# An opening by quarters of the inner dimension, in a written order, and narrower modulation products

## The chip, the cores and the metric

The kernel runs on one core of one Trainium2 chip. Times are device microseconds of one execution; the time before is the median of three runs, 1925.92 us (1925.78 to 1932.32).

## What is computed

Two sequences, a prompt of 256 tokens and a sample of 512, each with a conditioning vector `c`, go through a trunk of two layers with 1024 channels:

```python
for l in range(DEPTH):
    mod = jax.nn.silu(c) @ adaln_w[l] + adaln_b[l]           # 1024 -> 6 x 1024
    sh1, sc1, g1, sh2, sc2, g2 = [t[:, None, :] for t in jnp.split(mod, 6, axis=-1)]
    h = rmsnorm(x, norm_g[l, 0]) * (1 + sc1) + sh1
    y = mlstm_mixer(h, ...) if l % 2 == 0 else swa_mixer(h, ...)
    x = x + g1 * y
    h = rmsnorm(x, norm_g[l, 1]) * (1 + sc2) + sh2
    x = x + g2 * conv_ffn(h, ...)
return rmsnorm(x, final_g)
```

The mixer of layer 0 is a bidirectional mLSTM with four heads. From `h` it takes q, k, v and an output gate (1024 columns each) and 16 gate columns; the gates go through a log-sigmoid, cumulative sums and running maxima, whose results weigh the scores q k^T of each head. All of it is in float32.

## The kernel before

Activations lie transposed, channels on the 128 partitions in eight chunks (`KC`), tokens along the free dimension: the prompt at columns 0 to 255, the sample at 256 to 767. A float32 operand of a large matmul is split into a rounded high part (ScalarE) and the rest (VectorE) by `fp_copy_split`, L221, and each product is done as three: high x high, high x low, low x high. Modulated activations are held split in `hh` and `hl` (the tiles zh and zl in the profile), weights in `whi` and `wlo`. All matmuls but transposes and the feed-forward's are recorded at L219. A weight half (`load`, 512 KB) holds 128 output columns of all eight chunks: one "tile" of a projection is 24 products for a sequence.

The program is written in Python and ordered per engine by a scheduler that works with a cost model; the order in the text is a priority, not the order of execution. Tiles are taken from pools with a fixed number of buffers: six large `slab`s, five `raw` landing buffers, three `whi` and three `wlo`, four PSUM banks `ps` and four `pa`.

The opening is `first`, L1281. It loads x by ranges (sample columns 256 to 511, 512 to 767, then the prompt) and, between them, the 8 MB of the first 2048 columns of layer 0's modulation matrix (shift and scale of the mixer) in sixteen pieces of 128 rows by 1024 columns. `adaln`, L354, multiplies each piece by `silc`, silu(c) of both sequences padded to 32 columns, in two products of 512 columns, each into a strip of 32 partitions of one PSUM bank; all eight chunks of the inner dimension have to be summed before the bank is copied, transposed and added to the bias as `mod` and `gain`. `Norm`, L85, squares on ScalarE, adds six chunks on GpSimd, sums over partitions on PE (L119), takes the power on GpSimd (L126) and spreads the factor with PE (L131); `scaled`, L485, multiplies x by it, and `modulate`, L490, applies gain and shift and splits. When that is done for the sample, `window`, L276, runs the first three tiles (gates, two of head 0's q) over both ranges of the sample and then the prompt. Head 0's k (two tiles) and v (`gemmN`, L297) follow in `mlstm`, L559, and beside them the chain of the gates: table loads, scans (L599 to L606), a trip through DRAM (`mrows`) and masks on GpSimd (L626), without which no score of head 0 can be weighed.

The other modulation columns are worked off beside the heads, as generators advanced at fixed places: `fillp` does layer 0's remaining 4096 columns on PE with `adaln`; `fill` does layer 1's on VectorE with `adaln_v`, L415, one step being two operations of 128x1024.

Of the kernel before, what the change touches and what calls it, by code (L numbers as in the profile page):

```python
# [140 lines left out]
class Net:  # L141
# [103 lines left out]

    def halves(self, u):
        for h in range(2):
            yield h, self.split(self.load(u, h))

    def step(self, gen, n=1):  # L250
        for _ in range(n):
            next(gen, None)

# [7 lines left out]
    def gemmT_steps(self, w, q, act=None):  # L261
        s0, s1 = SEQS[q]
        wh, wl = (t.rearrange("p (k m) -> p k m", k=KC) for t in w)
        ps = self.ps()
        o = ps[:, : s1 - s0]
        for k in range(KC):
            if act is None:
                ah, al = self.hh[:, k, s0:s1], self.hl[:, k, s0:s1]
            else:
                ah, al = act(k, s0, s1)  # L270
            self.mm(o, wh[:, k], ah, k == 0, False)
            self.mm(o, wh[:, k], al, False, False)
            self.mm(o, wl[:, k], ah, False, k == KC - 1)
            yield o

    def window(self, items):  # L276

        bank = {}
        for rng in RANGES:
# [3 lines left out]
            for i, (w, consume) in enumerate(items):  # L283
# [10 lines left out]
                if c1 == s1:  # L294
                    consume(q, bank[i, q][:, : s1 - s0])

# [57 lines left out]
    def adaln(self, l, th, first=False):  # L354
        nc = self.nc
        hold = None

        def fetch(i):
            nonlocal hold
            k, h = divmod(i, 2)  # L360
            c0 = th * 2048 + h * 1024
            src = self.io["adaln_w"][l, k * P : (k + 1) * P, c0 : c0 + 1024]
            if k < 2 or not first:
                return self.raw(src)
            z = (i - 4) % 3
            if z == 0:
                hold = self.slab([P, 3, 1024])
            nc.sync.dma_start(hold[:, z], src)
            return hold[:, z]

        if not first:
            part = fetch(0)
            yield
        ps = self.ps()
        for i in range(2 * KC):
            k, h = divmod(i, 2)
            cur = fetch(i) if first else part
            if not first and i < 2 * KC - 1:
                part = fetch(i + 1)
            for g in range(2):  # L380
                r0 = 32 * (2 * h + g)
# [3 lines left out]
            if i < 2 * KC - 1 and (h or not first):  # L385
                yield
        sb = self.stg.tile([P, 2, 256], F32, tag="raw", name=self.nm("sb"), bufs=5)
        sb = [sb[:, z] for z in range(2)]
        nc.vector.tensor_copy(sb[0], ps[:, :256])
        nc.scalar.copy(sb[1], ps[:, 256:])  # L390
        pt = self.ps()
        for b in range(4):
            nc.tensor.transpose(
                pt[:, b * P : (b + 1) * P], sb[b // 2][:, (b % 2) * P : (b % 2 + 1) * P], self.ident
            )
        src = pt.rearrange("p (b g s) -> p g b s", b=4, g=4)[:, :, :, 0:2]
        dst = self.mod[l][:, th * 16 : (th + 1) * 16, :].rearrange("p (g b) s -> p g b s", g=4)
        ab = self.cst(AB + 48 * l + 16 * th, 16).rearrange("p (g b) -> p g b", g=4)
        for s in range(2):
            nc.vector.tensor_tensor(dst[:, :, :, s], src[:, :, :, s], ab, ALU.add)  # L400
        i = {0: 0, 2: 1}.get(th)
        if i is not None:
            c0 = 8 if i == 0 else 32
            for s in range(2):
                nc.vector.scalar_tensor_tensor(
                    self.gain[l][i][:, :, s],
                    self.mod[l][:, c0 : c0 + 8, s],
                    1.0,
                    self.cst(NG + (2 * l + i) * 8, 8),
                    ALU.add,  # L410
                    ALU.mult,
# [77 lines left out]

    def modulate(self, xt, rng, l, i):  # L490
        c0, c1, q = rng
        for c in range(KC):
            x = xt[c // 4][:, c % 4, c0:c1]
            self.nc.vector.tensor_scalar(
                x, x, self.gain[l][i][:, c, q : q + 1], self.mod[l][:, 24 * i + c, q : q + 1], ALU.mult, ALU.add
            )
            self.fp_copy_split(self.hh[:, c, c0:c1], self.hl[:, c, c0:c1], x)
# [61 lines left out]
    def mlstm(self, pool, gw, xt):  # L559
# [22 lines left out]
        qt0 = self.slab([P, 2, 2, T], R)  # L582
# [3 lines left out]
        norm = Norm(self, xt, PROMPT, self.modulated(0, 0), KC)  # L586
        for c in range(KC):
            norm.square(c)
        self.start(PROMPT, norm.stages())
        self.window(ws)  # L590
# [846 lines left out]
```

## Time and profile before

| | |
|---|---|
| median of the runs | 1925.92 us |
| profiled execution | 1921.48 us, span 1919.4 us |
| PE busy | 1836.2 us (96%) |
| DVE busy | 1387.2 us (72%) |
| ACT busy | 909.8 us (47%) |
| POOL busy | 559.6 us (29%) |
| chain that ended last | PE 80%, DVE 6%, issue 5%, DMA 3%, POOL 3% |

The profile covers one execution. A row of a timeline gives the start and the length in us, the engine, the source line, the operation, the tiles written and read, their shapes, how many records were merged, and in brackets how long the engine had been idle and what released it. PE is the matmul unit, PEld its weight loads, DVE VectorE, ACT ScalarE, POOL GpSimd. A float32 product on PE that is not split beforehand leaves two records, and some records can be missing. Matmuls are pipelined: the distance between two starts is what one costs, not the length in its row.

### The profile page before, as it was taken

The page shows a single profiled execution, that of the slowest core. Times are in us where ns is not written, and L with a number is a line of the kernel's source. Part 1 is how long each engine was busy: PE and PEld are TensorE (multiplying, and loading weights), DVE is VectorE, ACT ScalarE, POOL GpSimd, SP SyncE. Part 2 cuts the span into 40 slices and gives each one's busy share as a digit, 9 for nine tenths or more (in the row PEclk, how much of TensorE's full clock was granted, in tenths as well). Part 3 has the DMA queues.
Part 4 walks back from the last instruction along what each step waited for, and adds up shares of the span by engine and source line. Part 5 has one row for each costly group of instructions (what it writes and reads, how often), then busy time and mean ns, then how long its engine had stood idle before and what let it go on. Part 6 is the DMA issues. An engine that isn't in the chain of part 4 may idle for free.

```text
span 1919.4 us, 28838 instructions
## 1 busy us (share of the span) xinstructions
PE 1836.2 (96%) x11142; PEld 1662.5 (87%) x11142; DVE 1387.2 (72%) x2243; ACT 909.8 (47%) x1826; POOL 559.6 (29%) x438
## 2 busy tenths in 40 slices
PE   7999999999999999999999999999899999999997
PEld 4977786888988899999999998779898999999996
DVE  4765566686589867777777765774798777777776
ACT  3444433343456444444444554773565444444443
POOL 2101001022253433333331311342533333333324
PEclk9999999999999999999999999999999999999998
DMA  8344456446212222222222321122222222222211
GB/s 327 107 149 133 148 167 211 134 146 220 83 55 78 69 64 67 66 66 67 67 69 86 99 90 52 40 87 78 82 73 66 66 66 67 73 70 67 66 34 66
DMA packets 63956, 183.41 MB, mean 96 GB/s; under 512 B 6135, under 2 KB 23799, under 8 KB 63820
## 3 DMA queue, kind: packets, MB, share of 16 engines
q1 hardware_dynamic: 63820, 181.58, 29.7%
q8 instruction: 87, 1.43, 0.3%
q14 instruction: 49, 0.40, 0.1%
HBM read 175.13 MB, written 6.43 MB: 95 GB/s over the span
## 4 chain that ended last, share of the span: by engine, by line
PE 80%; DVE 6%; issue 5%; DMA 3%; POOL 3%; ACT 2%; SPq 0%; POOLq 0%; ACTq 0%; DVEq 0%
PE pa L219 25%; PE ps L219 22%; PE ps L1050 10%; PE ps L1051 10%; PE ps L1052 10%; PE pa L908 2%; DMA raw<-in_adaln_w_dram 1%; DVE wlo L226 1%; DVE slab L517 1%; POOL nt L107 1%; PE pa L1050 1%; PE pa L1051 1%; ACT whi L225 1%; PE pa L1052 1%; DMA slab<-in_x_dram 1%
## 5 line engine op out<-in xcount | busy, mean ns | idle before, releaser
L225 ACT CAST whi<-raw 128x1024 fp32r<-128x1024 f32 x243 | 254.6, 1049 | 413.0 <-PE pa L219 203.5
L226 DVE TENSOR_TENSOR wlo<-raw,whi 128x1024 fp32r<-128x1024 f32 x243 | 335.3, 1381 | 132.9 <-ACT whi L225 131.4
L219 PE MATMUL pa<-slab,whi 128*128 128x256 f32 (+1 forms) x1472 | 344.7, 331 | 4.8 <-DVE slab L517 4.8
L219 PEld LDWEIGHTS pa<-slab,whi 128*128 128x128 f32 x1472 | 251.1, 188 | 31.8 <-DVE slab L517 6.3
L517 DVE SCALAR_TENSOR_TENSOR slab<-pa,mod,slab 128x256 f32<-128x256 f32 (+1 forms) x368 | 207.4, 592 | 68.8 <-PE pa L219 68.6
L219 PE MATMUL ps<-zh,whi 128*128 128x256 f32 (+2 forms) x688 | 227.6, 334 | 7.4 <-ACT whi L225 4.9
L219 PE MATMUL pa<-slab,wlo 128*128 128x256 f32 (+1 forms) x736 | 233.3, 329 | 0.0
L219 PE MATMUL ps<-zh,wlo 128*128 128x256 f32 (+2 forms) x688 | 227.5, 333 | 3.3 <-DVE wlo L226 3.3
L219 PE MATMUL ps<-zl,whi 128*128 128x256 f32 (+2 forms) x688 | 228.7, 334 | 0.7 <-DVE zl L480 0.7
L1050 PE MATMUL ps<-zh,whi 128*128 128x384 f32 x504 | 171.2, 340 | 17.7 <-ACT ps L1113 16.7
L1052 PE MATMUL ps<-zh,wlo 128*128 128x384 f32 x504 | 169.4, 336 | 0.1
L1051 PE MATMUL ps<-zl,whi 128*128 128x384 f32 x504 | 169.4, 336 | 0.0
L1081 POOL TENSOR_TENSOR raw<-raw,raw 128x512 f32<-128x512 f32 x44 | 60.1, 1366 | 307.5 <-DVE wlo L226 262.4
L219 PEld LDWEIGHTS pa<-slab,wlo 128*128 128x128 f32 x736 | 138.3, 188 | 12.9 <-DVE wlo L226 0.6
L219 PEld LDWEIGHTS ps<-zh,whi 128*128 128x128 f32 x688 | 130.5, 191 | 21.9 <-ACT whi L225 6.5
L219 PEld LDWEIGHTS ps<-zh,wlo 128*128 128x128 f32 x688 | 131.0, 191 | 16.6 <-DVE wlo L226 4.4
L219 PEld LDWEIGHTS ps<-zl,whi 128*128 128x128 f32 x688 | 131.2, 191 | 11.6 <-issue 1.7
L1202 POOL TENSOR_TENSOR slab<-slab 128x772 f32<-128x772 f32 x44 | 87.6, 1991 | 178.9 <-DVE slab L1153 177.8
L1152 DVE SCALAR_TENSOR_TENSOR slab<-slab,cstt,slab 128x771 f32<-128x771 f32 x88 | 107.0, 1218 | 26.7 <-ACT slab L1150 26.7
L436 DVE SCALAR_TENSOR_TENSOR ada<-raw,silc,ada 128x1024 f32<-128x1024 f32 x84 | 109.5, 1336 | 18.4 <-DMA raw<-in_adaln_w_dram 18.4
L1153 DVE SCALAR_TENSOR_TENSOR slab<-slab,cstt,slab 128x771 f32<-128x771 f32 x88 | 121.0, 1376 | 0.7
L1050 PEld LDWEIGHTS ps<-zh,whi 128*128 128x128 f32 x504 | 94.7, 188 | 25.7 <-ACT ps L1113 21.8
(273 smaller groups left out, 4191.9 us busy)
## 6 DMA issues: line engine op xcount, KB each, us to landing
raw<-in_w_dram SPq DMA_DIRECT2D x206, 512.0 KB, 3.7
raw<-in_adaln_w_dram SPq DMA_DIRECT2D x84, 512.0 KB, 4.5
slab<-in_x_dram SPq DMA_DIRECT2D x12, 512.0 KB, 8.3
slab<-in_adaln_w_dram SPq DMA_DIRECT2D x12, 512.0 KB, 10.3
slab<-mrows SPq DMA_DIRECT2D x8, 384.0 KB, 5.1
xs<-slab SPq DMA_DIRECT2D x6, 512.0 KB, 2.9
bt<-brow SPq DMA_DIRECT2D x16, 192.0 KB, 3.1
slab<-xs SPq DMA_DIRECT2D x6, 512.0 KB, 8.1
```

Of the source, the lines that this page charges most:

```text
L219: self.nc.tensor.matmul(out, lhsT, rhs, start=start, stop=stop)
L225: nc.scalar.copy(hi, src)
L226: return nc.vector.tensor_tensor(lo, src, hi.bitcast(F32), ALU.subtract)
L436: stt(acc[:, s], row, w, acc[:, s], ALU.mult, ALU.add)
L517: self.nc.vector.scalar_tensor_tensor(x, o, self.mod[l][:, gc + c, q : q + 1], x, ALU.mult, ALU.add)
L1050: mm(o, wh[:, k], hi[k], start=start and k == 0, stop=False, skip_group_check=True)
L1051: mm(o, wh[:, k], lo[k], start=False, stop=False, skip_group_check=True)
L1052: mm(o, wl[:, k], hi[k], start=False, stop=k == 3, skip_group_check=True)
L1081: tt(q[0], q[2], q[0], ALU.subtract)
L1152: stt(y[:, 1:], u[:, :-1], w(0), y[:, 1:], ALU.mult, ALU.add)
L1153: stt(y[:, :-1], u[:, 1:], w(2), y[:, :-1], ALU.mult, ALU.add)
L1202: nc.gpsimd.tensor_tensor(y, y, yrow[:, j], ALU.mult)
```

## The change

The first 2048 modulation columns come from a second copy of the matrix, `ada0`, packed on the host so that quarter z (four loads of 512 KB) holds all rows for channels 256z to 256z+255 of shift and scale. For each quarter `opening` does `adaln_z` (eight products of 512 columns in four strips, a copy, four products with `sel` that add up the strips and transpose), modulates and splits two chunks of the sample, and does these two chunks' products of the first three tiles, all 512 columns of the sample at once. Then come the prompt's norm, two more tiles (head 0's k) of the sample, and outside of the written part the five tiles of the prompt. PE, ACT and DVE keep the order of the text in `opening`. The x loads of the sample and all quarters with the first weights are issued ahead. `window` stays for layer 1.

The remaining columns of layer 0 go through `adaln_g`: four groups of 1024 columns instead of two of 2048, a step being a piece of 128x1024 as before, but in four products of 256 columns in four strips instead of two of 512 in two. Steps of `fill` move: none in head 0's values, one more at the second block of each sequence's outputs in each head. `modulated` queues a chunk's low part behind the next chunk's product, and the prompt's scores are split in one piece.

```diff
+    def apart(self, src, pool):
+        w = [[pool.tile([P, 640], R, tag="PT", name=self.nm("wp"), bufs=8)[:, :512] for _ in range(2)] for _ in range(2)]
+        for j in range(2):
+            self.fp_copy_split(w[0][j], w[1][j], src[:, 512 * j : 512 * (j + 1)])
+        return w
...
+    def products(self, o, w, ks, cols):
+        for k in ks:
+            ah, al = self.hh[:, k, cols], self.hl[:, k, cols]
+            self.mm(o, w[0][k], ah, k == 0, False)
+            self.mm(o, w[0][k], al, False, False)
+            self.mm(o, w[1][k], ah, False, k == KC - 1)
+
+    def opening(self, xt, units, loads, pool, consume):
+        nc = self.nc
+        sample, prompt = (slice(*s) for s in SEQS)
+        ws, bank = [], []
+        for rng in RANGES[:2]:
+            Norm(self, xt, rng, self.scaled).run()
+        for z in range(4):
+            self.adaln_z(z, units[z], pool)
+            cs = (2 * z, 2 * z + 1)
+            xs = [xt[c // 4][:, c % 4, sample] for c in cs]
+            for c, x in zip(cs, xs):
+                nc.vector.tensor_scalar(
+                    x, x, self.gain[0][0][:, c, 0:1], self.mod[0][:, c, 0:1], ALU.mult, ALU.add
+                )
+            for c, x in zip(cs, xs):
+                self.fp_copy_split(self.hh[:, c, sample], self.hl[:, c, sample], x)
+            for i in range(3):
+                if z == 0:
+                    bank.append(self.ps())
+                    ws.append(self.blocks(self.split(loads[i]) if i else self.apart(loads[i], pool)))
+                self.products(bank[i], ws[i], cs, sample)
+        norm = Norm(self, xt, PROMPT, self.modulated(0, 0))
+        for c in range(KC):
+            norm.square(c)
+        stages = norm.stages()
+        next(stages)
+        for i in range(2):
+            w = self.load(U_MIN + 1, i)
+            ws.append(self.blocks(self.apart(w, pool) if i else self.split(w)))
+        for i in range(3):
+            consume[i](0, bank[i])
+        bank += [self.ps() for _ in range(2)]
+        self.products(bank[3], ws[3], range(4), sample)
+        next(stages)
+        self.products(bank[3], ws[3], range(4, KC), sample)
+        consume[3](0, bank[3])
+        for _ in stages:
+            pass
+        self.products(bank[4], ws[4], range(KC), sample)
+        consume[4](0, bank[4])
+        return ws
...
+    def adaln_z(self, z, units, pool):
+        nc = self.nc
+        ps = self.pa()
+        for k in range(KC):
+            r0 = 32 * (k % 4)
+            self.mm(ps[r0 : r0 + 32], self.silc[:, k, :], units[k // 2][:, k % 2], k < 4, k > 3)
+        sb = pool.tile([P, 640], F32, tag="E", name=self.nm("sb"), bufs=2)
+        nc.scalar.copy(sb[:, :512], ps)
+        pt = self.pa()[:, :8]
+        for b in range(4):
+            self.mm(pt[:, 2 * b : 2 * b + 2], sb[:, b * P : (b + 1) * P], self.sel, True, True)
+        src = pt.rearrange("p (i b s) -> p i b s", i=2, b=2)
+        for i in range(2):
+            c = 8 * i + 2 * z
+            ab = self.cst(AB + c, 2).unsqueeze(2).to_broadcast([P, 2, 2])
+            nc.vector.tensor_tensor(self.mod[0][:, c : c + 2, :], src[:, i], ab, ALU.add)
...
+    def adaln_g(self, l, grp):
...
+        for k in range(KC):
+            cur = part
+            if k < KC - 1:
+                part = fetch(k + 1)
+            for g in range(4):
+                r0 = 32 * g
                 self.mm(
-                    ps[r0 : r0 + 32, :], self.silc[:, k, :], cur[:, g * 512 : (g + 1) * 512], k == 0, k == KC - 1
+                    ps[r0 : r0 + 32, :256], self.silc[:, k, :], cur[:, g * 256 : (g + 1) * 256], k == 0, k == KC - 1
                 )
...
-            for c in range(KC):
-                t = self.tmp([P, c1 - c0])
-                sh = self.mod[l][:, 24 * i + c, q : q + 1]
-                nc.vector.scalar_tensor_tensor(t, x(c), self.gain[l][i][:, c, q : q + 1], pr, ALU.mult, ALU.mult)
-                hi, lo = self.hh[:, c, c0:c1], self.hl[:, c, c0:c1]
-                nc.scalar.activation(hi, t, AF.Identity, bias=sh)
-                nc.vector.scalar_tensor_tensor(lo, t, sh, hi.bitcast(F32), ALU.add, ALU.subtract)
+            ts = []
+            for c in range(KC + 1):
+                if c < KC:
+                    ts.append(self.tmp([P, c1 - c0]))
...
+                if c:
+                    b = c - 1
+                    self.behind = nc.vector.scalar_tensor_tensor(
+                        self.hl[:, b, c0:c1], ts[b], self.mod[l][:, 24 * i + b, q : q + 1],
+                        self.hh[:, b, c0:c1].bitcast(F32), ALU.add, ALU.subtract,
+                    )
...
-        ws = [(gw, gates)] + [(w, keep(qt0, 0, c)) for c, w in self.halves(U_MIN)]
-        self.load_x(io["x"], RANGES[2:], xt)
...
-        self.start(PROMPT, norm.stages())
-        self.window(ws)
-        nc.scalar.preload_act_table_set("natural_log_exp_and_others")
+        with self.tc.manual_schedule(engines={eng.PE, eng.Activation, eng.DVE}):
+            ws = opening(consume)
+        behind = self.behind
+        self.tc.keep_in_program_order(
+            nc.scalar.preload_act_table_set("natural_log_exp_and_others")
+        )
+        for w, f in zip(ws, consume):
+            o = self.ps()[:, :256]
+            self.products(o, w, range(KC), slice(*SEQS[1]))
+            f(1, o)
...
+                    if i == 1:
+                        with self.tc.issue_after(behind.ins):
+                            self.step(self.fill)
...
-        xt = self.load_x(x, RANGES[:1])
-        ada = self.adaln(0, 0, True)
-        steps = lambda n: [next(ada, None) for _ in range(n)]
-        Norm(self, xt, RANGES[0], self.scaled).run()
-        steps(4)
-        self.load_x(x, RANGES[1:2], xt)
...
+        xt = self.load_x(x, RANGES[:2])
...
+        units = [self.quarter_loads(0, pool)]
+        loads = [self.raw(self.io["wg"]), self.load(U_MIN, 0)]
+        units.append(self.quarter_loads(1, pool))
+        loads.append(self.load(U_MIN, 1))
+        units += [self.quarter_loads(z, pool) for z in (2, 3)]
+        self.load_x(x, RANGES[2:], xt)
...
-        self.fillp = chain(self.adaln(0, 1), self.adaln(0, 2))
+        self.fillp = chain(*(self.adaln_g(0, grp) for grp in range(2, 6)))
...
+    a0 = inp["adaln_w"][0][:, :2048].reshape(KC, P, 2, 4, 256)
+    arr["ada0"] = np.ascontiguousarray(a0.transpose(1, 3, 0, 2, 4).reshape(P, 4 * 4096))
```

More of the change, by code (lines that the diff above doesn't have):

```diff
@@ L351, in save_x, with quarter_loads @@
             self.nc.sync.dma_start(dst[:, 4 * i : 4 * i + 4, c0:c1], xt[i][:, :, c0:c1])
-    def adaln(self, l, th, first=False):
-        nc = self.nc
[L356 to L373, printed above, removed]
-        ps = self.ps()
[L375 to L381, printed above, removed]
+    def quarter_loads(self, z, pool):
+        out = []
+        for u in range(4 * z, 4 * z + 4):
+            if u < 12:
+                if u % 3 == 0:
+                    self.hold = self.slab([P, 3, 1024])
+                part = self.hold[:, u % 3]
+            elif u < 14:
+                if u == 12:
+                    self.hold = pool.tile([P, 2, 1024], F32, tag="ada", name=self.nm("ada"), bufs=1)
+                part = self.hold[:, u - 12]
+            else:
+                part = self.stg.tile([P, 1024], F32, tag="raw", name=self.nm("raw"), bufs=5)
+            self.nc.sync.dma_start(part, self.io["ada0"][:, u * 1024 : (u + 1) * 1024])
+            out.append(part.rearrange("p (k c) -> p k c", k=2))
+        return out
@@ L384, in adaln @@
                 )
-            if i < 2 * KC - 1 and (h or not first):
+            if k < KC - 1:
                 yield
[L387 to L395, printed above, removed]
@@ L396, in adaln @@
[L396 to L398 removed]
+        sb = self.stg.tile([P, 2, P], F32, tag="raw", name=self.nm("sb"), bufs=5)
+        nc.vector.tensor_copy(sb[:, 0], ps[:, :P])
+        nc.scalar.copy(sb[:, 1], ps[:, P : 2 * P])
+        pt = self.ps()[:, : 2 * P]
+        for b in range(2):
+            nc.tensor.transpose(pt[:, b * P : (b + 1) * P], sb[:, b], self.ident)
```

93 lines of the change are left out of this document (44 added, 49 removed).

## The prediction

> **What bounds the kernel now.** I read the head of the page first, then the busy time of each engine by stage.
>
> ```profile
> span 1919.4 us, 28838 instructions
> 0.00:40.00 40.00, 26.24 (x122) 11.73 (x122) 14.74 (x41) 14.06 (x36) 8.90 (x16) 0.99 0.97 365
> 40.00:87.00 47.00, 47.00 (x328) 44.94 (x327) 39.38 (x69) 24.43 (x42) 3.28 (x1) 0.94 0.33 105
> 105.00:380.00 275.00, 262.88 (x1652) 211.52 (x1650) 170.39 (x301) 109.07 (x291) 19.59 (x12) 0.99 0.49 157
> ```
>
> After the window's length come the busy times of PE, its weight loads, DVE, ACT and POOL, then granted clock, DMA share and GB/s. From 40 us on TensorE is busy 94 to 100% of each stage, so time is won by giving it less work, or by starting its work earlier. Only the first 40 us are different: DMA is 97% busy, and TensorE's 26 us are modulation products and norm sums. The timeline shows where that opening ends and what follows.
>
> ```profile
> 33.24 1.05 PE L219 MATMUL ps<-slab,silc 128*32 128x512 f32 x4 [0.26 <-DMA slab<-in_adaln_w_dram]
> 42.46 0.56 PE L219 MATMUL ps<-zh,whi 128*128 128x256 f32 x1
> 61.80 0.60 ACT L228 ACTIVATE slab<-ps 128x512 fp32r<-128x512 f32 x1 [2.28 <-PE ps L219]
> 87.52 0.39 PE L219 MATMUL ps<-whi,zh 128*128 128x256 f32 x1 [0.45 <-DVE slab L226]
> ```
>
> The last modulation piece lands at 33.2; dense sample products run from 42.5. At 61.8 ScalarE evicts the third tile of the sample, and at 87.5 the values of head 0 begin, when five tiles (gates, two of q, two of k) are done for both sequences. The new opening ends with the same five tiles, so 87.5 is my yardstick.
>
> **Part one: the start of the new opening.** Both sample norms now stand ahead of everything on PE, in written order. The rows of the old norms price the new ones:
>
> ```profile
> 8.69 1.34 ACT L103 ACTIVATE nt<-slab 128x256 f32<-128x256 f32 x4 [0.37 <-DMA slab<-in_x_dram]
> 7.78 3.94 POOL L107 TENSOR_TENSOR nt<-nt,nt 128x256 f32<-128x256 f32 x5 [7.34 <-ACT nt L103]
> 13.12 2.72 PE L219 MATMUL pa<-inv,nt 128*128 128x2 f32 x12
> 25.26 1.50 PE L219 MATMUL pa<-inv,nt 128*128 128x2 f32 x12
> 16.12 0.72 POOL L126 TENSOR_TENSOR nr<-nr,mhalf 128x2 f32<-128x2 f32 x1 [4.39 <-DVE nr L125]
> 17.63 1.22 PE L219 MATMUL pa<-kct,nr 128*128 128x128 f32 x4
> 18.95 2.74 DVE L487 TENSOR_TENSOR slab<-slab,pa 128x256 f32<-128x256 f32 x8 [2.92 <-PE pa L219]
> 18.79 3.46 PE L219 MATMUL ps<-slab,silc 128*32 128x512 f32 x16
> ```
>
> The twelve sums took 2.72 us early and 1.50 later: PE starts slow, and I use the early prices. First norm: adds end at 11.7, sums 14.5, power 15.5, broadcast 16.8, scaling on DVE 19.6. Second: sums 16.8 to 19.5, its mean behind the first scaling 19.8, power 20.6, broadcast 21.9. By then the first quarter is there. It is the third to sixth MB in the queue, and the windows give 410 GB/s:
>
> ```profile
> 24.00:28.00 4.00, 3.77 (x27) 2.02 (x26) 1.73 (x2) 0.00 (x0) 1.85 (x3) 1.00 1.03 410
> 40.00:44.00 4.00, 4.00 (x20) 4.00 (x20) 4.00 (x13) 4.00 (x10) 0.00 (x0) 0.50 0.37 147
> ```
>
> x in 8.7 to 11.3, then 2 MB in 5.1 us: about 16.4. Later quarters, with the weights between, land by about 24, 30 and 35 us.
>
> **Part two: one quarter.** PE does, in order, eight modulation products, four narrow transposing sums, then 18 products of 512 columns; z+1's modulation stands behind z's products. Prices:
>
> ```profile
> 192.49 1.07 PE L219 MATMUL ps<-raw,silc 128*32 128x512 f32 x8
> 193.49 0.63 PE L219 MATMUL pa<-slab,PT 128*128 128x258 f32 x3
> 119.58 0.39 PE L219 MATMUL ps<-zh,whi 128*128 128x512 f32 x1
> 120.26 0.39 PE L219 MATMUL ps<-zh,whi 128*128 128x512 f32 x1
> 35.70 0.26 DVE L400 TENSOR_TENSOR mod<-ps,cstt 128x16 f32<-128x16 f32 x2 [0.94 <-PE ps L393]
> 35.91 0.25 DVE L405 SCALAR_TENSOR_TENSOR gain<-mod,cstt 128x8 f32<-128x8 f32 x2
> 36.12 5.26 DVE L494 TENSOR_SCALAR slab<-slab,gain,mod 128x256 f32<-128x256 f32 x16
> 62.43 0.69 DVE L229 SCALAR_TENSOR_TENSOR slab<-ps,slab 128x512 fp32r<-128x512 f32 x1 [0.36 <-ACT slab L228]
> ```
>
> - Modulation: a product leaves two records, so the x8 row is four products in four strips of the array. PE went on 1.0 us later, so eight products take 2.0.
> - Eviction of 512 columns by ACT: 0.6 (the row at 61.80).
> - Four sums with two columns, eight records at 1.50/12: 1.0, and 0.1 to finish.
> - Three small DVE operations at 0.13: 0.4. Modulating 512 columns: 5.26/16 is 0.33 per 256, so 0.7. High part on ACT: 0.6.
> - 18 products: three in 0.68 (119.58 to 120.26), so 4.1; the first tile also waits for low parts at 0.69 each: 4.4.
>
> Sum: 2.0 + 0.6 + 1.1 + 0.4 + 0.7 + 0.6 + 4.4 = 9.8 us, against 5.1 us for its load. So from the second quarter on the data wait for PE's chain, not PE for the data. The first quarter pays early prices: modulation 3.5 (25.4), eviction (26.0), sums 1.8 (27.8), small operations and modulating (28.9), two low parts and three weight splits on DVE (1.4 + 3 x 1.25), last products 0.7: about 35.5. Three more quarters at 9.8 end the sample's three tiles at 64.9; the old ones end at 61.8 or before.
>
> **Part three: the rest of the opening.** Rows before ran 24 products of 256 columns at 0.12, 2.9 us, and 24 of 512 in 5.4. The fourth tile waits for its split behind the prompt's squares (0.9), then 5.4; sums 1.5; broadcast 0.6; fifth tile 5.4, which hides the prompt's modulation; five prompt tiles 14.4. 64.9 + 28.2 = 93.1 against 87.5: **+5.6 us**. DVE's clearing of the scan rows waits for a slab of quarter two and may fall into a chain (up to 2.6); I take 0, since DVE is idle while PE does the products.
>
> Behind it the gates' chain could show. It now starts at 81.7, after one prompt tile.
>
> ```profile
> 65.56 0.47 ACT L572 ACTIVATE slab<-pa,cstt 36x256 f32<-36x256 f32 x1
> 65.15 2.48 DVE L436 SCALAR_TENSOR_TENSOR ada<-raw,silc,ada 128x1024 f32<-128x1024 f32 x2 [2.02 <-DMA raw<-in_adaln_w_dram]
> 68.92 1.28 ACT L593 ACT_TABLE_LOAD   x1
> 90.51 3.68 POOL L626 TENSOR_TENSOR slab<-slab,kct 128x768 f32<-128x768 f32 x2 [40.87 <-DMA slab<-mrows]
> 105.83 4.46 PE L219 MATMUL pa<-slab,slab 128*128 128x512 f32 x18
> ```
>
> From gates to masks took 28.6 us, with 2.5 of layer 1's modulation and two table loads in it that go: masks at 105 to 110.3. Scores begin 18.3 after the values (87.5 to 105.8): 111.4. Hidden, cost 0; without that cover up to 5.
>
> **Part four: narrow modulation products.** Groups 2 to 5 need 32 steps either way.
>
> ```profile
> 100.00:380.00 280.00, 29.08 (x128) 4.35 (x128) 72.08 (x62) 0.00 (x0) 0.99 0.49 156
> 110.22 1.05 PE L219 MATMUL ps<-raw,silc 128*32 128x512 f32 x4
> 111.20 0.97 PE L219 MATMUL pa<-slab,slab 128*128 128x512 f32 x3
> ```
>
> The first is the window of the instructions on silc alone: 128 records, 64 products, 29.1 us. Most steps stand alone like that at 110.22: two products in two strips hold PE 0.98. A narrow step has four products of 256 columns in four strips: half of the 1.0 of four at 512, and 0.05 between: 0.55. 32 x 0.55 = 17.6, a gain of 11.5. Some steps stand where PE waits anyway (4% of this stage), so I take **-10**. The bounds: nothing, if a step is held by its sixteen weight loads and products rather than by its columns, and -11.5. Groups end four times, not twice, each with a copy and transposes that PE may wait for:
>
> ```profile
> 234.64 0.84 PE L393 MATMUL ps<-kct,sb 128*128 128x128 f32 x4
> 237.69 0.50 PE L219 MATMUL ps<-zh,whi 128*128 128x512 f32 x1 [2.21 <-ACT whi L225]
> ```
>
> Between 0 and 2.2 each; near the copy's own 0.4: **+1** for two. Layer 1's modulation on DVE keeps its steps, but three leave head 0's values and eight go into the heads' outputs, ahead of the denominators of the second block. The 2.5 us there sit on a DVE busy 62% of the stage; I take 0, from -3 (less in the output gate) to +5 (the wait of 2.2 above grows). Joining the prompt's score splits and the new order in `modulated` save instructions off PE: 0 to -1, taken 0.
>
> **The sum.** +5.6 - 10 + 1 = -3.4 on the profiled execution of 1921.48 us (span 1919.4), giving 1918.1. The median shown, 1925.92, is 4.4 above that execution, so the same step from it gives **1922.5**.
>
> **The rivals.**
> (a) *The quarters are shorter than my chain.* PE's own work is 2.0 + 1.1 + 4.1 = 7.2, and with overlap a quarter may take 7.5: three times 2.3 and 3 in the first make 10. Then the sum is -13.4: 1912.5. For it speaks idle ACT and DVE; against it that each step of the chain needs the one before.
> (b) *The clock falls in each quarter's lull.* This ends on the other side. Between modulation and products PE has 3.4 us with only two-column sums. Before, the same sort of stretch (33.2 to 42.5) brought the granted clock to 0.50 at 40 to 44. At half clock 18 products take 4.1 more; for four quarters +16, so -3.4 + 16 = +12.6: 1938.5. It decides once more than two quarters fall; against it, the clock stayed 1.00 at 24 to 28 with short gaps. The Trainium skill ("TensorE: Matmul & The Clock Gate", "HAM oscillation — how this bites in real kernels") says the same against splitting the inner dimension: do all pieces of it before waiting on a transfer, or the array goes cold each time. By that rule the sum would be the rival's; the trace agrees for one longer lull and shows none of 3.4.
> (c) *The narrow steps save nothing*, held by their issue: +5.6 + 1: 1932.5. Against it, four products' weights are loaded in 0.16 us, and PE went on after 1.0:
>
> ```profile
> 192.49 0.16 PEld L219 LDWEIGHTS ps<-raw,silc 128*32 128x32 f32 x8
> ```
>
> **How the numbers follow.** Half a per cent, 9.6 us, is about what a measurement can tell from no change: faster is below 1916.3, slower above 1935.5. My forecast has 0.50 (with an error of some 8 us: 0.09 faster, 0.39 same, 0.02 slower); (a) 0.19, nearly all faster (0.17, 0.02); (b) 0.18 (0.02 same, 0.16 slower); (c) 0.13 (0.08 same, 0.05 slower). Sums: 0.26, 0.51, 0.23. The range takes in (a), less 4 for unknown costs, and most of (b): 1908 to 1939.
>
> **What would show it.** Right: four bursts of 18 products of 512 columns, 9 to 11 us apart, with PE idle some 3 us in each; the third ends near 55, the fourth near 65; values of head 0 start near 93; silc's products after 100 us fall from 29 to some 18 us. Wrong: bursts 5 to 7 us apart, or clock at 0.5 through the opening, or steps of silc that still hold PE 1 us, or idle of several us before the score products.

## The result, and the profile after

The changed kernel takes 1937.92 us (median of 9 runs, 1934.55 to 1941.33) against 1927.69 us for the kernel before, run beside it (9 runs, 1923.08 to 1932.32): a ratio of 1.0052, 95% interval 1.0039 to 1.0064. It is slower, by 10 us; forecast were 1922.5 us and a small gain. The profiled execution took 1937.19 us.

The busy time by stage shows where. The cuts are the first product of head 0's values and the first product of the output projection. Columns: window, length, busy time and instructions of PE, weight loads, DVE, ACT and POOL, granted clock, DMA share, GB/s. Before:

```profile
0.00:87.52 87.52, 73.31 (x449) 56.68 (x449) 54.64 (x110) 38.97 (x77) 12.19 (x17) 0.96 0.62 223
87.52:462.45 374.93, 358.23 (x2260) 295.89 (x2260) 241.97 (x397) 146.31 (x373) 46.46 (x31) 0.99 0.49 158
462.45:1919.45 1457.00, 1404.69 (x8434) 1309.90 (x8434) 1090.60 (x1738) 724.55 (x1377) 500.98 (x390) 0.99 0.23 72
```

After:

```profile
span 1935.2 us, 28966 instructions
0.00:101.07 101.07, 74.74 (x384) 57.35 (x385) 42.91 (x90) 36.30 (x70) 13.93 (x22) 0.93 0.51 186
101.07:476.55 375.48, 353.89 (x2391) 303.36 (x2389) 254.89 (x410) 148.28 (x369) 46.02 (x31) 0.97 0.50 164
476.55:1935.21 1458.66, 1405.50 (x8434) 1311.38 (x8434) 1086.87 (x1736) 722.34 (x1375) 501.67 (x390) 0.99 0.22 71
```

Head 0's values start at 101.07 instead of 87.52: the opening costs 13.6 us. PE's idle time grew by 12.1 (length minus busy time: 26.3 against 14.2), its busy time by 1.4, and the granted clock fell from 0.96 to 0.93. In the middle stage the narrow products were to win some 10 us; it is as long as before, and its granted clock fell from 0.99 to 0.97. The last stage has no part of the change; its 1.7 us are within what one execution differs from another.

**The quarters.** Timeline of the kernel after, one quarter of four:

```profile
50.24 1.92 PE L219 MATMUL pa<-slab,silc 128*32 128x512 f32 x16
52.29 0.58 ACT L446 COPY sb<-pa 128x512 f32<-128x512 f32 x1 [7.67 <-PE pa L219]
52.93 1.05 PE L219 MATMUL pa<-sel,sb 128*128 128x2 f32 x8 [0.76 <-ACT sb L446]
54.02 0.23 DVE L454 TENSOR_TENSOR mod<-pa,cstt 128x4 f32<-128x4 f32 x2 [8.60 <-PE pa L219]
54.28 0.16 DVE L456 SCALAR_TENSOR_TENSOR gain<-mod,cstt 128x4 f32<-128x4 f32 x1
54.48 1.00 DVE L330 TENSOR_SCALAR slab<-slab,gain,mod 128x512 f32<-128x512 f32 x2
55.06 1.14 ACT L225 CAST zh<-slab 128x512 fp32r<-128x512 f32 x2 [2.19 <-DVE slab L330]
55.71 1.29 DVE L226 TENSOR_TENSOR zl<-slab,zh 128x512 fp32r<-128x512 f32 x2 [0.23 <-ACT zh L225]
55.73 0.79 PE L219 MATMUL ps<-zh,wp 128*128 128x512 f32 x1 [1.75 <-ACT zh L225]
...
60.46 0.63 PE L219 MATMUL ps<-zl,whi 128*128 128x512 f32 x1
60.89 0.60 PE L219 MATMUL ps<-zh,wlo 128*128 128x512 f32 x1
...
62.02 0.39 PE L219 MATMUL ps<-zh,whi 128*128 128x512 f32 x1
62.25 0.39 PE L219 MATMUL ps<-zl,whi 128*128 128x512 f32 x1
...
62.80 1.07 PE L219 MATMUL pa<-ada,silc 128*32 128x512 f32 x8
```

The reader sees the predicted chain: modulation, copy, narrow sums, three small DVE operations, the modulating of two chunks, high part, products. From 50.24 to the first product it takes 5.49 us; the forecast had 5.4. But the 18 products then take 7.07 us (55.73 to 62.80), not 4.4: up to 61.3 their starts are 0.43 apart, afterwards 0.23. The windows of 4 us say why (granted clock is the third number from the end):

```profile
50.00:54.00 4.00, 3.22 (x26) 1.39 (x24) 0.00 (x0) 0.58 (x1) 0.00 (x0) 1.00 0.00 0
54.00:58.00 4.00, 2.27 (x5) 1.54 (x6) 2.69 (x7) 1.14 (x2) 0.00 (x0) 0.56 0.00 0
58.00:62.00 4.00, 4.00 (x12) 3.12 (x11) 0.00 (x0) 0.00 (x0) 0.00 (x0) 0.58 0.00 0
62.00:66.00 4.00, 3.21 (x25) 1.29 (x23) 0.00 (x0) 0.58 (x1) 0.00 (x0) 1.00 0.08 9
```

In the 3.5 us before the burst PE does nothing but the two-column sums; the burst starts at half clock and gets the full clock back after 5.6 us. The other quarters show the same, in part shorter: from the first to the fourth the 18 products take 6.95, 6.09, 7.07 and 5.90 us. In the first quarter it shows in the starts alone, 0.43 apart until 37.1; the granted clock stands at 1.00 there.

**The narrow steps.** The window of silc's instructions after 100 us, and one step in the timeline:

```profile
100.00:380.00 280.00, 18.85 (x236) 6.63 (x236) 89.94 (x74) 0.00 (x0) 0.97 0.50 167
```

```profile
141.15 0.64 PE L219 MATMUL ps<-raw,silc 128*32 128x256 f32 x8
141.72 0.50 PE L219 MATMUL ps<-zh,whi 128*128 128x512 f32 x1
```

29.08 us became 18.85, and PE goes on 0.57 us after a step's start. That gain is there; something else in the stage took it back.

### The profile page after: what moved, and what is told of

Same layout as the page of the kernel before. It is cut to its first block, busy times and chain, and to the rows that moved or that the text cites. A ratio compares the mean times of both kernels' runs of the same rounds, so it can differ in the third digit from the quotient of the medians.

```text
span 1935.2 us, 28966 instructions
## 1 busy us (share of the span) xinstructions
PE 1834.1 (95%) x11206; PEld 1672.1 (86%) x11206; DVE 1384.7 (72%) x2235; ACT 906.9 (47%) x1814; POOL 561.6 (29%) x443
## 5 line engine op out<-in xcount | busy, mean ns | idle before, releaser
L226 DVE TENSOR_TENSOR wlo<-raw,whi 128x1024 fp32r<-128x1024 f32 x241 | 331.4, 1378 | 127.4 <-ACT whi L225 126.0
L219 PE MATMUL ps<-zh,whi 128*128 128x256 f32 (+2 forms) x656 | 222.3, 343 | 10.2 <-ACT whi L225 8.9
L219 PE MATMUL ps<-zh,wlo 128*128 128x256 f32 (+2 forms) x656 | 221.9, 341 | 1.9 <-DVE wlo L226 1.9
L219 PE MATMUL ps<-zl,whi 128*128 128x256 f32 (+2 forms) x656 | 223.0, 341 | 0.4 <-DVE zl L568 0.4
L219 PEld LDWEIGHTS ps<-zh,whi 128*128 128x128 f32 x656 | 126.2, 194 | 25.8 <-ACT whi L225 11.7
L219 PEld LDWEIGHTS ps<-zh,wlo 128*128 128x128 f32 x656 | 126.2, 193 | 13.9 <-DVE wlo L226 3.0
L219 PEld LDWEIGHTS ps<-zl,whi 128*128 128x128 f32 x656 | 126.7, 193 | 12.6 <-issue 1.5
L1133 PEld LDWEIGHTS ps<-zh,whi 128*128 128x128 f32 x504 | 95.1, 189 | 24.5 <-ACT ps L1196 20.6
## 6 DMA issues: line engine op xcount, KB each, us to landing
slab<-in_ada_dram SPq DMA_DIRECT2D x12, 512.0 KB, 10.2
```

Of the source, the lines that this page charges most:

```text
L219: self.nc.tensor.matmul(out, lhsT, rhs, start=start, stop=stop)
L226: return nc.vector.tensor_tensor(lo, src, hi.bitcast(F32), ALU.subtract)
L1133: mm(o, wh[:, k], hi[k], start=start and k == 0, stop=False, skip_group_check=True)
```

## The experiments

All ran in four sets of five rounds beside the kernel before, whose median in the sets was 1927.25, 1926.34, 1926.07 and 1926.75 us; the last set (fill_one_back, fill_early_in_head1, fill_early_old_opening) ran on another chip than the first three. Every diff is cut to its core.

### One part alone, one part undone

**narrow_only**: the kernel before with the narrow products.

```diff
-        self.fillp = chain(self.adaln(0, 1), self.adaln(0, 2))
+        self.fillp = chain(*(self.adaln_g(0, grp) for grp in range(2, 6)))
```

> The kernel before with the narrow modulation steps alone (four groups of 1024 columns, four products of 256 columns in four strips); opening, fill steps and the rest as before. Theory 1 (a narrow step holds the matmul unit 0.55 us instead of 0.98, and nearly all of it is on the path): about 10 us faster than the kernel before, 1918. Theory 2 (the time saved comes back as waits for the 512 KB pieces and as half clock): no change to 4 us faster, 1924 to 1928.

Measured: 1912.42 us (1909.65 to 1916.02), ratio 0.9928 [0.9913, 0.9944]. The narrow products win 14.8 us on their own, more than the 10 expected.

**fill_as_before**: the changed kernel with layer 1's steps where they were.

```diff
-                    if h:
-                        self.step((self.fill, self.fillp)[t % 2])
+                    if t % 2 == 0:
+                        with self.tc.issue_after(behind.ins):
+                            self.step(self.fill)
+                    elif h:
+                        self.step(self.fillp)
...
-                    if i == 1:
-                        with self.tc.issue_after(behind.ins):
-                            self.step(self.fill)
```

> The changed kernel with the steps of layer 1's modulation put back where they were (every second row of head 0's values too, none in the heads' outputs). Theory 1 (the moved steps block the denominators on the vector engine at the end of each head and let the clock fall; that ate the gain of the narrow steps): 6 to 8 us faster than the changed kernel, about 1931. Theory 2 (the ends of the heads wait for the transfers of the pieces whatever stands there): within 2 us of the changed kernel, 1936 to 1940.

Measured: 1926.44 us (1921.79 to 1930.86), 11.5 below the changed kernel, with the middle stage down from 375.5 to 362.5 us. The moved steps, which the forecast put at 0, cost as much as the narrow products win.

**opening_only**: the changed kernel with the wide products (`adaln`) and the old places of the steps, so that the opening alone is left of the change.

> The changed kernel with the old wide modulation steps (two of 512 columns) and the steps of layer 1's modulation where they were: of the change only the opening (and the two small edits to the splits) is left. Theory 1 (the parts add: opening +13.6 us by the start of head 0's values, narrow steps -14, moved fill steps +11.5): 1940 to 1943, 13 to 15 us slower than the kernel before. Theory 2 (the later opening start is partly hidden by the gates' chain and the heads): under 8 us slower.

Measured: 1943.40 us (1938.91 to 1945.29), ratio 1.0084 [1.0059, 1.0109]: 17 us above the kernel before. It differs from fill_as_before only in the wide products, so on the new opening the narrow ones win 17.0 (1943.40 against 1926.44). The three parts taken singly, 17.1 - 14.8 + 11.5 = 13.8, come near the whole, 10 to 12.

### The opening: lull and clock

**quarter_ahead**: the next quarter's modulation products stand ahead of this quarter's tiles, its sums behind the first of them.

```diff
+            if z < 3:
+                nxt = self.adaln_z(z + 1, units[z + 1], pool)
+                next(nxt)
             for i in range(3):
+                if i == 1 and z < 3:
+                    next(nxt, None)
...
         nc.scalar.copy(sb[:, :512], ps)
+        yield
```

> The changed kernel with the next quarter's eight modulation products and their copy put ahead of this quarter's tiles, and its strip sums behind the first tile; nothing else. Theory 1 (the opening is long because each quarter's chain stands between bursts and the clock falls in the lull): bursts about 7.5 us apart instead of 11.5 to 12.6, the fourth ends near 58 instead of 74, total 13 to 18 us less than the changed kernel, 1920 to 1925. Theory 2 (what is won in the opening is lost behind it, because the gates' chain and the transfers set when head 0 ends): opening shorter by as much, total less by under 5 us.

Measured: 1924.73 us (1918.96 to 1929.44), 13.2 below the changed kernel. Windows of this kernel, the opening and four microseconds of it, and from its timeline two quarters' starts:

```profile
0.00:86.70 86.70, 67.36 (x384) 52.59 (x385) 42.84 (x90) 36.25 (x70) 14.01 (x22) 0.96 0.61 217
```

```profile
46.00:50.00 4.00, 4.00 (x28) 2.21 (x26) 2.46 (x5) 1.15 (x2) 0.00 (x0) 1.00 0.00 0
```

```profile
41.08 2.26 PE L219 MATMUL pa<-slab,silc 128*32 128x512 f32 x16
...
48.55 1.07 PE L219 MATMUL pa<-ada,silc 128*32 128x512 f32 x8
```

Between 46 and 50 PE is busy without a break and at full clock, the quarter from 41.08 is 7.47 long, and head 0's values start at 86.7. Filling the lull with the next quarter's own work takes away both the idle time and the slow products; it does not tell how much is which.

**clock_kept**: the lull filled with idle products (their results are not used), one group of four ahead of the sums and two behind them.

```diff
+    def burn(self, o, units, n):
+        for _ in range(n):
+            for k in range(4):
+                self.mm(o[32 * k : 32 * k + 32], self.silc[:, k, :], units[k // 2][:, k % 2], True, True)
```

> The changed kernel with three groups of four idle products per quarter (on data of the same quarter, results unused) in the two lulls of each quarter, so that the matmul unit is busy while it would wait. Theory 1 (half clock after each lull is what lengthens the bursts from 4.4 to 6 or 7 us): bursts of about 4.5 us, granted clock 1.00 through the opening, quarters 10.3 us apart instead of 11.5 to 12.6, about 5 us less in all, 1933. Theory 2 (the bursts are slow because they wait for splits): bursts as long as they are, quarters longer by the idle products, 1 to 3 us more in all.

Measured: 1938.52 us (1928.86 to 1944.82), no gain in the median. In the profiled execution, the fastest of its eleven, the windows from the second quarter on are at full clock and a burst is shorter (windows, then timeline):

```profile
54.00:58.00 4.00, 3.80 (x23) 2.24 (x16) 1.96 (x4) 1.14 (x2) 0.00 (x0) 1.00 0.01 4
58.00:62.00 4.00, 4.00 (x33) 1.83 (x31) 0.00 (x0) 0.18 (x1) 0.00 (x0) 1.00 0.00 0
```

```profile
54.94 0.49 PE L219 MATMUL ps<-zh,wp 128*128 128x512 f32 x1
...
59.74 1.07 PE L219 MATMUL pa<-ada,silc 128*32 128x512 f32 x8
```

The 18 products take 4.80 us here (54.94 to 59.74) where the changed kernel took 7.07, and a quarter is 10.35 long. So the slow burst is the clock's doing, and the clock falls because of the lull: that much the one profile shows. Why the other executions of this kernel spread over 16 us and the median stays where it was is open.

**ahead_splits_early**: quarter_ahead with the steps of layer 1 at their old places, and the three weight splits written ahead of the first quarter.

> As the run with both repairs, and the first three weight splits are queued behind the norms instead of inside the first quarter, where the third ends at about 36 us. Theory 1 (the first quarter is set by the vector engine's splits, 9 us from first to last product): the first quarter's products end 4 to 5 us earlier, and so does the rest, 1907 to 1909. Theory 2 (the third and fourth quarter's loads, at 30 and 35 us, set the pace then): 1 to 2 us better, 1911 to 1912.

Measured: 1914.41 us (1911.52 to 1918.46), 2.4 above ahead_and_fill, its partner below: the order of the splits is not where time is lost.

### The moved steps: which of them, and why

**fill_none**: the changed kernel without the eight added steps; head 0's three stay away. **fill_removed_only**: the same, with four steps added in the output gate's first block, so that none is left over at the end.

> The changed kernel without the added steps of layer 1's modulation at the second block of the heads' outputs, and still without those in head 0's values: eight steps fewer beside the heads, so the rest ends in the output gate. Theory 1 (the added steps, which stand ahead of the denominators on the vector engine, cost the 11.5 us): as fast as with the old places, 1924 to 1929. Theory 2 (taking three steps from head 0's values is what costs, because they pile up later): as slow as the changed kernel or slower, 1936 to 1942.

> The changed kernel, without the eight new steps and without head 0's three; four additional steps in the first block of the output gate keep the chain from being left over at the end. Theory 1 (the added steps cost): 1924 to 1929 us, stage near 363. Theory 2 (the missing steps cost): 1934 to 1940, stage 371 or more.

Measured: 1942.31 us (1936.96 to 1948.73) and 1942.80 us (1940.63 to 1944.86). Taking the added steps away does not help, it costs 5 more. My first theory, that 2.5 us of VectorE ahead of a block's denominators hold up TensorE, fell. In the first of the two, steps are left over at the end, which could cost by itself; the second is free of that.

**fill_behind_outputs**: the eight added steps behind the operations that scale the block's output.

> The changed kernel, with each of the eight new steps issued behind the two operations that scale the second block's output, not ahead of its denominators. Theory 1 in its narrow form (the step delays the denominators of its own block): 1924 to 1930 us. If any place of these steps costs as much, or if the missing steps of head 0 do: 1934 to 1940.

Measured: 1938.08 us (1932.65 to 1941.07). Their place in the block does not matter.

**fill_both_places**: head 0's three steps back, the eight added ones kept. **fill_moved_old_opening**: the kernel before with narrow products and the moved steps.

> The changed kernel, with the three steps of layer 1's modulation in head 0's values put back and the eight new ones in the heads' outputs kept (the chain of steps ends earlier in the output gate). Theory 1 (the added steps cost: 2.5 us of VectorE ahead of a block's denominators, TensorE waits, its clock falls): it stays at 1934 to 1940 us, and the stage from head 0's values to the output projection at about 374. Theory 2 (the missing steps cost: without the three in head 0 the loads, and with them all later steps, fall at other moments): 1924 to 1929, stage near 363.

> The kernel before with the narrow modulation products and with the steps of layer 1's modulation moved as in the change; the old opening. If the moved steps cost the same whatever the opening: 1922 to 1926 us, 10 to 13 above the narrow products alone (1912.4). If the cost comes only with the new opening's load order: 1911 to 1915.

Measured: 1927.06 us (1922.83 to 1931.91) and 1929.05 us (1919.04 to 1935.68). So the missing three of head 0 cost all of it, the added eight nothing, and it has nothing to do with the new opening: there too the move costs 16.6 (1929.05 against 1912.42), more than expected.

What do three steps in head 0 do? The timelines have it. A group of layer 1's modulation is eight rows into one accumulator (`ada`, one buffer). The first step only loads; the eighth row and the products that empty the accumulator belong to the ninth, and only behind these products can the next group's first row be taken. Rows of the kernel after, VectorE's on `ada` and the first such products on PE:

```profile
153.79 2.48 DVE L521 SCALAR_TENSOR_TENSOR ada<-raw,silc,ada 128x1024 f32<-128x1024 f32 x2 [1.14 <-DMA raw<-in_adaln_w_dram]
...
196.64 1.07 PE L219 MATMUL ps<-ada,ones 128*32 128x512 f32 x8
...
198.64 1.41 DVE L519 TENSOR_SCALAR ada<-raw,silc 128x1024 f32<-128x1024 f32 x2
```

VectorE has the eighth row done at 156, far ahead of its place in the text, since the scheduler lets an engine with room run ahead. PE has no room: the products stay at the ninth step's place in its order, and VectorE has no row to work on for 42 us (32 in fill_one_back below). In the written order that was the last of head 1's six steps in q and k (three of head 0, then six). With head 0's three gone and two added in its outputs, it is the first one in head 1's values. Two more sets of steps tell this place (theory A) from the work itself (theory B):

**fill_one_back**: one of head 0's three steps back. **fill_early_in_head1** and **fill_early_old_opening**: two more steps in head 1's q and k and none in head 0's values, on the new and on the old opening.

```diff
-                        if q <= c or h > 1:
+                        if h:
                             self.step(self.fill)
```

> The changed kernel, with one of head 0's three steps put back, the eight new ones kept. Theory A (place of the group's end): the ninth step is head 1's last one before its values, as in the kernel before; first products on the accumulator 84 us or less after head 0's values start; 1924 to 1930 us. Theory B (work done in head 0's values): only a third comes back, 1932 to 1937.

> The changed kernel, with two more of layer 1's steps in head 1's projections of q and k (none goes back to head 0's values). Theory A (place of the group's end: the ninth step ends the first group of eight, its two-row accumulator is freed only there, and the change lets that step fall into head 1's values, 95 us after head 0's values start instead of 84, so that later steps are pushed onto VectorE at the heads' ends): the ninth step is now within head 1's projections, the first products on the accumulator come 70 to 86 us after head 0's values start, and the time is 1924 to 1930. Theory B (head 0's values are the one place where VectorE has room for these steps): it stays at 1935 to 1941.

> The kernel before with the narrow products and the moved steps (1929 us), with two more steps in head 1's projections of q and k. Theory A (place of the group's end): it falls to 1911 to 1917. Theory B (work done in head 0's values): it stays at 1926 to 1931.

Measured: 1927.60 us (1923.59 to 1930.25), 1929.40 us (1926.82 to 1932.33) and 1912.08 us (1909.29 to 1914.72): all three as theory A has them, with the group's end in the first two at 84.8 and 87.9 us, a little past the expected 84 and 86. The same rows in fill_one_back:

```profile
152.18 2.47 DVE L521 SCALAR_TENSOR_TENSOR ada<-raw,silc,ada 128x1024 f32<-128x1024 f32 x2
...
185.32 1.06 PE L219 MATMUL ps<-ada,ones 128*32 128x512 f32 x8
...
186.79 1.41 DVE L519 TENSOR_SCALAR ada<-raw,silc 128x1024 f32<-128x1024 f32 x2
```

All runs with narrow products, by the distance from the start of head 0's values to the first products on the accumulator (from the timelines; stage is the middle stage of the profiled execution):

| kernel | distance, us | stage, us | median, us |
|---|---|---|---|
| fill_both_places | 71.2 | 363.2 | 1927.06 |
| fill_early_old_opening | 80.0 | 361.0 | 1912.08 |
| ahead_splits_early | 82.9 | 361.2 | 1914.41 |
| ahead_and_fill | 83.5 | 361.5 | 1912.00 |
| narrow_only | 83.7 | 364.1 | 1912.42 |
| fill_as_before | 84.4 | 362.5 | 1926.44 |
| fill_one_back | 84.8 | 362.5 | 1927.60 |
| fill_early_in_head1 | 87.9 | 368.5 | 1929.40 |
| fill_behind_outputs | 94.5 | 371.3 | 1938.08 |
| clock_kept | 95.2 | 374.2 | 1938.52 |
| the kernel after | 95.6 | 375.5 | 1937.92 |
| quarter_ahead | 96.5 | 372.7 | 1924.73 |
| fill_moved_old_opening | 96.8 | 380.2 | 1929.05 |
| fill_removed_only | 111.1 | 378.9 | 1942.80 |
| fill_none | 111.7 | 371.8 | 1942.31 |

Up to 85 us the stage takes 361 to 364, from 94 on 371 to 380, and at 87.9 it lies between. That the place of the steps decides, and not work done in head 0's values, is shown by fill_one_back, fill_early_in_head1 and fill_early_old_opening. But every run that brings the first group's end forward brings the later ones forward with it, so which group's end costs is not shown.

One rival can be seen in the traces: the kernels without a step in head 0's values, but for fill_early_old_opening, wait 2.6 to 4.8 us near the end of head 0 for a piece of layer 0's matrix (4.76 us, up to 157.28, in the kernel after). fill_early_in_head1 has this wait too, 2.59, and is fast again, so it is not the whole cost; whether its longer stage comes from it is not shown.

How the lateness turns into 10 us is read from traces, and no run takes it apart. The third group of the kernel after ends at 301.6 (290.1 in fill_one_back), close to the end of a head, and the rows of the next group meet the next head's weights there (timeline, then windows):

```profile
308.62 2.47 DVE L521 SCALAR_TENSOR_TENSOR ada<-raw,silc,ada 128x1024 f32<-128x1024 f32 x2
...
309.15 1.04 ACT L225 CAST whi<-raw 128x1024 fp32r<-128x1024 f32 x1
310.25 0.60 PE L219 MATMUL ps<-zh,whi 128*128 128x512 f32 x1 [1.90 <-ACT whi L225]
...
311.41 1.22 DVE L226 TENSOR_TENSOR wlo<-raw,whi 128x1024 fp32r<-128x1024 f32 x1
```

```profile
308.00:312.00 4.00, 2.10 (x14) 1.28 (x6) 3.58 (x5) 2.26 (x5) 0.00 (x0) 0.81 0.69 259
312.00:316.00 4.00, 3.45 (x9) 2.65 (x9) 4.00 (x7) 0.17 (x2) 0.83 (x1) 0.50 0.82 244
```

PE waits 1.90 us for the next head's weights, their low part stands behind 2.5 us of layer 1's rows, and the products that follow are at half clock (0.50 from 312 to 316). In fill_one_back the same product waits 1.21 and the clock stays:

```profile
307.48 0.50 PE L219 MATMUL ps<-zh,whi 128*128 128x512 f32 x1 [1.21 <-ACT whi L225]
```

```profile
307.00:311.00 4.00, 3.34 (x15) 2.66 (x16) 4.00 (x7) 1.04 (x4) 0.00 (x0) 1.00 0.72 235
311.00:315.00 4.00, 4.00 (x23) 3.47 (x22) 4.00 (x10) 1.82 (x4) 0.00 (x0) 1.00 0.85 279
```

What these rows show is a small part of the loss. Counted from the start of head 0's values, the kernel after is 2.2 us behind fill_one_back at this product, 5.0 at the first product of the output gate (392.39 and 386.81) and 13.0 at the end of the stage: some 8 us are lost in the output gate. In these 25 us of it PE waits and runs below full clock, and in fill_one_back it does neither (the kernel after first):

```profile
400.00:425.00 25.00, 22.46 (x121) 18.21 (x121) 21.57 (x32) 11.34 (x27) 7.45 (x5) 0.86 0.53 169
400.00:425.00 25.00, 25.00 (x151) 22.34 (x150) 22.84 (x31) 9.68 (x22) 6.50 (x6) 1.00 0.52 176
```

And the loss does not hang on the half clock at this product: in fill_behind_outputs, as slow as the kernel after, it waits 2.17 us and the clock stays at 1.00 from 308 to 316.

### Both repairs together

**ahead_and_fill**: quarter_ahead and fill_as_before in one.

> The changed kernel with both repairs: next quarter's modulation ahead of this quarter's tiles, and the steps of layer 1's modulation at their old places; narrow steps kept. Theory 1 (the two costs lie in different stages and add): 1937.9 - 13.2 - 11.5 = 1913, as fast as the old opening with narrow steps (1912.4). Theory 2 (both repairs cure the same lull): no better than either alone, 1922 to 1925.

Measured: 1912.00 us (1909.51 to 1913.95), ratio 0.9923 [0.9901, 0.9945]: 14 us below the kernel before, 26 below the changed one. The two repairs add up (13.2 + 11.5 = 24.7). But narrow_only, with the old opening, is as fast (1912.42): the opening by quarters, at its best here, is worth nothing against the old one.

## Why the prediction was right or wrong

- **The yardstick and the chain of a quarter: right.** The first modulation starts at 22.2 (21.9 worked out), and copy, sums, small operations and splits together take what the rows of before gave, to 0.1 us (5.49 against 5.4).
- **18 products in 4.4 us: the first step that failed.** They took 7.07 us in the quarter shown and 6.95, 6.09 and 5.90 in the others, and the quarters follow at 11.5, 12.6 and 11.4 us instead of 9.8; the first ended at 38.72 instead of 35.5. Together 9.3 us too short, of which the slow products are some 8; the rest of the opening came 1.3 shorter than its 28.2. So the opening's term is +13.6 and not +5.6. This is rival (b)'s mechanism, which I gave 0.18; the argument against it, full clock between 24 and 28 "with short gaps", did not hold for 3.5 us with nothing in them but two-column sums. The rival's price of 4.1 a quarter was too high: from 1.5 to 2.7 is lost against 4.4, since the clock comes back within the burst. The Trainium skill ("TensorE: Matmul & The Clock Gate", "HAM oscillation — how this bites in real kernels") advises to do all pieces of the inner dimension before a wait for a transfer, so that the array stays warm; the trace agrees in kind, though the waits here are for ACT and DVE. The Trainium skill's measure in the same section, no idle gap over some 3.4 us, is too wide for this trace if the two-column sums count as work: the longest idle time in each of the later three quarters is 1.75 us, and the clock falls. With the sums and the 0.7 to 0.8 us of idle before them the lull is 3.5 us, and no run tells which of the two counts.
- **Narrow steps -10: right in kind, too small.** Silc's products fell by 10.2 us, and narrow_only's middle stage is 10.8 shorter than the one before (364.1 against 374.9). But the medians fell by 14.8 and 17.0, past the bound of -11.5; what the 5 to 7 us beyond the forecast are is open. Rival (c) fell; rival (a)'s quarter of 7.5 us came only in quarter_ahead, with other work in the lull.
- **Group ends +1:** no run takes it apart from the steps.
- **Moved steps 0, from -3 to +5: the second step that failed, and the larger surprise.** They cost 11.5. I priced the steps where they arrive, 2.5 us of VectorE ahead of a denominator, and that costs nothing, as fill_both_places shows. I didn't ask what the steps do that leave: they advance a chain with one accumulator, and its first turn moved behind the rest of head 1's q and k. The buffer that the next step needs was not looked at. How the 11.5 us come about from there stays open, as said above.
- **The gates' chain hidden: right.** Scores start at 113.17 us, 12.1 behind the values, with PE at work until then.
- **The sum.** The forecast was +5.6 - 10 + 1 = -3.4. As measured it is +13.6 - 14.8 + 11.5 = 10.3, against 10.2 between the two medians. The opening and the moved steps were 8.0 and 11.5 too low, the narrow steps 4.8 too high. That the total came within a microsecond of rival (b)'s 1938.5, and that it lies inside the range, is chance: rival (b)'s mechanism accounts for about half of the miss, and the moved steps were in no rival.

## What to carry to other kernels

Splitting an inner dimension to start earlier cost time here as long as the matmul unit had no other work between the pieces: with the next piece's first products put into the lull, a quarter of this opening took some 7 us instead of 12, but even then the opening only came even with an opening that waits for all of its data. Of a background chain that is advanced step by step, look not only at what a step costs but at which step frees the chain's buffer, and keep that step's place when steps are moved: one of three steps put back recovered 10 of 11.5 us. And a part that wins (the narrow products) should be tried without the parts that came with it.

## What the runs showed of the hardware

- The length of a wait alone does not settle whether the granted clock falls. It halved after 1.75 us of idle behind a microsecond of two-column sums, and after waits of 1.90 and 2.56 us at heads' ends. But a wait of the same 2.56 us, behind the same products, left it at 1.00 in quarter_ahead, and one of 2.21 did so in the kernel before (at 237.69). What else decides is open. The kernel after, then quarter_ahead:

```profile
251.53 0.50 PE L219 MATMUL ps<-zh,whi 128*128 128x512 f32 x1 [2.56 <-ACT whi L225]
252.00:256.00 4.00, 4.00 (x17) 3.43 (x16) 4.00 (x6) 0.47 (x2) 0.00 (x0) 0.57 0.87 298
237.33 0.50 PE L219 MATMUL ps<-zh,whi 128*128 128x512 f32 x1 [2.56 <-ACT whi L225]
237.00:241.00 4.00, 3.67 (x20) 3.21 (x21) 3.69 (x6) 1.11 (x3) 0.16 (x1) 1.00 0.87 280
```

- In the later three quarters of the kernel after it took 3.5, 5.6 and 3.0 us of products for the full clock to come back.
- Four products of 256 columns in four strips hold PE 0.57 us where two of 512 in two strips held it 0.98: the time goes with the columns of one strip, to within 0.1 us.
- Idle products keep the clock at 1.00 from the second quarter on in the one profile that has them, yet gained nothing in the median of eleven runs. That is open.
